# Where loads, casts and sums stand near changes of stage, in a two-sequence encoder on one core

## The chip, the core and the metric

The kernel runs on one core of a Trainium2 chip. The metric is the device time of one execution in microseconds. Three timed runs of the kernel before gave a median of 1177.14 us (1176.59 to 1180.3).

## The reference

A trunk of two layers is applied to two sequences with shared weights: the short one, Q, has 512 positions, the long one, S, has 1024; both have 1024 channels, in float32.

```python
def even_layer(x, ...):                  # layer 1
    p = rms_norm(x, g_norm) @ w_in
    a_val, a_glu, f_in, a_z, f_z = split(p)          # 512 channels each
    a = depthwise_conv(a_val * sigmoid(a_glu), 31)
    a = silu(layer_norm(a)) * silu(a_z)
    f = einsum(fft2(f_in by 4 groups).real, w_four) * silu(f_z)
    return x + concatenate([a, f]) @ w_out

def odd_layer(x, ...):                   # layer 2
    u, bg, cg, z = split(rms_norm(x, g_norm) @ w_in)  # 1024 channels each
    v = depthwise_conv(cg * u, 3)
    return x + ((bg * v) * silu(z)) @ w_out

y = rms_norm(odd_layer(even_layer(x)), final_norm)
```

## The kernel before, in words

Activations lie with channels on the 128 partitions, in chunks of 512 positions: Q is one chunk, S two. Every operand of a product is split into a high and a low part in a reduced float32 format (`split`, L113, and `wsplit`, L143): ACT casts the high part, and a subtraction on DVE (activations) or POOL (weights) makes the low one. A tile of 128 output channels by 512 positions is then 3 x 8 = 24 matmuls (`project`, L174; high by high, high by low, low by high). Weights come in by DMAs of 256 KB that SP issues (`wraw`).

For S, the output projection of layer 1 and the input projection of layer 2 take both chunks and two weight tiles together, as a product of 2 x 2 blocks with seven multiplications instead of eight (`Pair`, L682): a product is 12 matmuls, the products are taken in the order 1, 5, 2, 6, 7, 4, 3, and accumulate in three PSUM tiles X, Z and Y. The weight side needs four sums of raw weight tiles (`sums`, L712, tiles `as` in the ring "T" of eight buffers), the activation side seven operands per block (`keep_op`, L809). X is reused: after products 1 and 6 it is read out into `xr` (layer 1, on DVE, L855) or `mc` (layer 2, on ACT by `taken`, L929) before the next product is added in it. The four pairs of layer 1's output are ma = 0, 2, 4, 6; the one with ma = 2 loads its raw weights early, into the ring "ld" (`room="ld"`).

The order of layer 1: GLU, Fourier input and the gates az and fz of Q and S, one after another. `l1_fz` makes the four fz tiles of Q, of which the last three are made just ahead of S's GLU (L1144); in S's first GLU (`l1_glu`, L343, j = 0) the tile of chunk 0 comes first, then that of chunk 1, which needs the normalised chunk 1: `x` is scaled on DVE (L285), cast to `nh` on ACT and subtracted to `nl` on DVE. The Fourier tables of S (`fourier_tables`, loads `tb`, casts `tbh`, subtractions `tbl`) follow in the program.

From then on a list of steps (`run`, L773) goes through: the layer 2 input tiles of Q for j = 0 to 5 (`l2_in`), the four pairs of layer 1's output for S, Q's tiles j = 6 and 7, Q's output (`l2_out`, tiles named `one` in PSUM), S's layer 2 pairs (`l2_two`), S's output. Side jobs are generators that advance at given steps: `out_ops_a/b/c` make the operands for the pairs of layer 1; `get_acts` (L1020) loads Q's normalised activations (parked in DRAM as `hm`, loaded as `ac`) and splits them to `ysh` and `ysl` for j = 6 and 7; `y2_acts_q` (also `ac`, from `yd`) does so for Q's output; `l2_ops` (L879) normalises S, makes the operands of products 1, 5, 2, 6, 7 and parks those of 4 and 3 in DRAM (`bd`); `prep_far` (L916) loads these (`bf`) and splits them (`bfh`, `bfl`); `l2_out` loads the residual tiles `xr2` and stores the sums (`x2`).

A list scheduler orders the instructions of each engine by simulated time and priority. `order` (L332) adds a dependency that sets the order of issue only. `pace` (L128) uses it: an instruction is placed behind the last evacuation of PSUM that `run` has seen.

Of the kernel before, what the change touches and what calls it, by code (L numbers as in the profile page):

```python
# [12 lines left out]
ALU = mybir.AluOpType  # L13
# [4 lines left out]
CH = 512  # L18
HF = 256
D = 1024  # L20
KD = D // P
# [42 lines left out]
def encoder(ctx: ExitStack, tc: tile.TileContext, xp, xs, w1, w1o, w2, w2o, wf4, par, cst, cdft, dft, outp, outs):  # L64
# [17 lines left out]
    def dp(s, width):  # L82
        return pool.tile([P, width], F32, name=nm(s), tag="dp", bufs=4)
# [25 lines left out]
    def tt(out, a, b, op, eng=nc.vector):  # L109
        ins = eng.tensor_tensor(out=out, in0=a, in1=b, op=op)  # L110
        return seen("now", ins) if eng is nc.vector else ins

    def split(src, tag, s, eng=nc.vector, paced=False):  # L113
        hi = pg(tag, s + "h", F32R)
        lo = pg(tag, s + "l", F32R)
        i = nc.scalar.copy(hi, src)
        j = tt(lo, src, hi.bitcast(F32), ALU.subtract, eng)
        if paced:
            pace(j)
        return hi, lo  # L120

    last = {}

    def seen(kind, ins):
        last[kind] = ins
        return ins

    def pace(ins):  # L128

        if "taken" in last:  # L130
            order(ins, last["taken"])

    def wtile(tag="wo"):
        return pool.tile([P, KD * P], F32R, name=nm("wo"), tag=tag, bufs=4)
# [197 lines left out]
    def order(ins, before):  # L332
        tc.add_manual_dep(ins.ins, before.ins.name, NOSYNC, reason="issue order")
# [6 lines left out]
        else:  # L340
            nc.scalar.activation(t, pq, func)

    def l1_glu(seq, h, skew=False, w0=None):  # L343
        for j in range(4):
            if seq is S:
                a = dp("a", seq.T + 2 * HALO)
            else:
                a = pool.tile([P, seq.T + 2 * HALO], F32, name=nm("ap"), tag="ap", bufs=4)
            nc.vector.memset(a[:, 0:HALO], 0.0)
            nc.vector.memset(a[:, HALO + seq.T:], 0.0)  # L350
            sig = [None] * seq.nc

            def do_glu(c, pq=None):
                if pq is None:
                    pq = project("glu", wg, h[c])
                t = sig[c] = pg("T", "sig")
                act_scaled(seq, t, pq, AF.Sigmoid)
                if seq.r is not None:
                    tt(t, t, seq.r, ALU.mult)

            def do_val(c, pq=None):
                if pq is None:
                    pq = project("val", wv, h[c])
                tt(a[:, HALO + c * CH:HALO + (c + 1) * CH], pq, sig[c], ALU.mult)

            if j == 0 and w0 is not None:
                pg_, pv_ = project_pair(w0, h[0])
                do_glu(0, pg_)
                do_val(0, pv_)
                seq.a.append(a)  # L370
                continue
            wg = load_w(w1, 4 + j)
            if skew and j == 0:
                wv = load_w(w1, j)
                for c in range(seq.nc):
                    do_glu(c)
                    do_val(c)
            else:
                for c in range(seq.nc):
                    do_glu(c)  # L380
                wv = load_w(w1, j)
                for c in range(seq.nc):
                    do_val(c)
            seq.a.append(a)
# [156 lines left out]
                if next(g, 0) == 0:  # L541
                    gens.remove(g)

    def l1_fz(seq, h, c, gs=range(4)):
        for g in gs:
            w = load_w(w1, 16 + g)
            pq = project("fz", w, h[c])
            t = pg("T", "fz")
            act_scaled(seq, t, pq, AF.Silu)
            f = seq.y1[c][4 + g]  # L550
            tt(f, f, t, ALU.mult, nc.gpsimd if seq is Q or c == 1 else nc.vector)
            if seq is S:
                seq.y1[c][4 + g] = park(f, "y1")
# [128 lines left out]
    class Pair:  # L682
# [29 lines left out]
        def sums(self):  # L712
            if self.left is None:
                a11, a21, a22, a12 = self.raw
                s1, s2, s3, s4 = [pg("T", "as") for _ in range(4)]
                tt(s1, a21, a22, ALU.add)
                tt(s2, s1, a11, ALU.subtract)
                tt(s3, a11, a21, ALU.subtract)
                tt(s4, a12, s2, ALU.subtract)
                self.left = {1: a11, 5: s1, 2: a12, 6: s2, 7: s3, 4: a22, 3: s4}  # L720

        def weight(self, p):
# [98 lines left out]
    def out_ops_b(seq, ops):  # L821

        for i in range(4):
            b11, b12 = [ld("y1", seq.y1[c][4 + i]) for c in range(2)]
            b21, b22 = [seq.y1[c][i] for c in range(2)]
            keep_op(ops, 2, b21, "ys", tag="H")
            tt(b12, b22, b12, ALU.subtract)
            keep_op(ops, 7, b12, "ys", tag="FQ")
            tt(b11, b12, b11, ALU.add)
            keep_op(ops, 6, b11, "ys", tag="H")  # L830
            tt(b21, b21, b11, ALU.subtract)
            yield 1
# [8 lines left out]
    def l1_out_two(seq, ops):  # L841
        acc = seq.sm2 = [SqSum(), SqSum()]

        def job(ma):
            at = {11: (0, ma), 12: (1, ma), 21: (0, ma + 1), 22: (1, ma + 1)}

            res = {}

            def pre():
                for ij in (11, 22, 12, 21):  # L850
                    c, m = at[ij]
                    res[ij] = pool.tile([P, CH], F32, name=nm("xr"), tag="ap", bufs=4)
                    nc.sync.dma_start(res[ij], seq.x[m, c])

            def before(ij):  # L855
                def run(x):
                    tt(res[ij], x, res[ij], ALU.add)
                    return res[ij]
                return run

            def after(ij):
                c, m = at[ij]

                def run(x, t=None):
                    t = res[ij]
                    tt(t, x, t, ALU.add)
                    sp = dram.tile([P, CH], F32, name=nm("x1d"), tag=f"x1d{seq.tag}{c}{m}", bufs=1)
                    nc.sync.dma_start(sp, t)
                    seq.x1[c][m] = sp
                    acc[c].add(t)  # L870
                return run

            return Pair(ops, w1o, ma, ma + 1, {ij: before(ij) for ij in (11, 12, 22)}, {ij: after(ij) for ij in at}, True,
                        wide=ma == 6, pre=pre, room="ld" if ma == 2 else None)

        return [job(ma) for ma in range(0, KD, 2)]
# [52 lines left out]
    def taken(tag):  # L929
        def run(x):  # L930
            t = pool.tile([P, CH], F32, name=nm("mc"), tag=tag, bufs=4) if tag == "ap" else pg(tag, "mc")
            nc.scalar.copy(t, x)  # L932
            return t
        return run

# [82 lines left out]
            yield 1  # L1018

    def get_acts(parked, acts, tag):  # L1020
        ts = [ld("ac", d) for d in parked[:4]]
        yield 1
        for n in range(0, KD, 4):
            new = []
            for i, t in enumerate(ts):
                acts.append(split(t, tag, "ys"))
                if n == 0:
                    new.append(ld("ac", parked[4 + i]))
            ts = new
            yield 1  # L1030

    def y2_acts_q(parked, acts):
# [2 lines left out]
                acts.append(split(parked[k] if k == KD - 1 else ld("ac", parked[k]), "F", "ys"))  # L1035
            yield 1

    def l2_out(seq, c, act, acc, ms, spilled=None, halves=None):
        def tile_of(m):
            def run(x):  # L1040
                t = ld("xr2", seq.x1[c][m], "ld" if halves is None else "FQ")
                tt(t, x, t, ALU.add)
                acc.add(t)
                if halves is None:
                    spilled.append(park(t, "x2"))
                else:
                    for h in range(2):
                        halves[h].append(t[:, h * HF:(h + 1) * HF])
            return One(w2o, m, act, run, kind=int(m == 0))
        return [tile_of(m) for m in ms]  # L1050
# [61 lines left out]
        nc.sync.dma_start(d, t)  # L1112
        return d

    def ld(s, src, tag="ld"):
        t = pg(tag, s)
        nc.sync.dma_start(t, src)
        return t


# [20 lines left out]
    second = norm_in(S, 1)  # L1141
    l1_fz(Q, hq, 0, range(1))
    hs.append(norm_in_rest(S, 1, *second))
    l1_fz(Q, hq, 0, range(1, 4))  # L1144
    l1_glu(S, hs, True)
    fourier_tables(S)
    l1_fin(S, hs)
    conv31(Q)
# [14 lines left out]
    def two_norms():  # L1163
# [15 lines left out]
        [t for j in range(n1) for t in l2_in(Q, hm, j, parked, j == 0)],  # L1179
        l1_out_two(S, yo),  # L1180
        [t for j in range(n1, KD) for t in l2_in(Q, hm2, j, parked, j == n1)],
        l2_out(Q, 0, act_q, acc_q, range(KD), out_q),
        [x for j in range(KD) for x in l2_two(S, ops, j)],
        l2_out(S, 0, act_s[0], acc_s[0], range(KD), out_s),
        l2_out(S, 1, act_s[1], acc_s[1], range(nd), halves=xt_e),
    ]
    at, seq = [], []
    for some in parts:
# [3 lines left out]
    run(seq, [  # L1192
        (4, 1, out_ops_a(S, yo)), (8, (0, 2, 4, 5, 6, 7, 8, 9, 10, 11, 12), two_norms()),
        (at[1], 1, out_ops_c(S, yo)),
        (at[2] - 6, 1, get_acts(kept, hm2, "H")),
        (at[2] + 1, (0, 1, 2, 4, 5, 8, 9, 10, 11), l2_ops(S, ops, far)),
        (at[2] + 2, (0, 1, 2, 3, 6), y2_acts_q(parked, act_q)),
        (at[4], 1, prep_far(ops, far)),
        (at[4] + 6, 1, norm_out(Q, 0, acc_q, out_q, "ld")),
        (at[5] - 4, 1, y2_acts(S, 0, act_s[0], "H")),  # L1200
        (at[5] + 1, 1, y2_acts(S, 1, act_s[1], "H")),
# [66 lines left out]
```

## Time and profile before

| | us |
|---|---|
| median of the timed runs | 1177.14 |
| the profiled execution | 1175.05 |
| its span | 1173.2 |
| PE busy | 1133.5 (97%) |
| DVE busy | 858.3 (73%) |
| ACT busy | 469.2 (40%) |
| POOL busy | 538.7 (46%) |

The rows of the profile's views name a line, an engine, an operation, and output <- inputs by the program's tile names, with the number of instructions. A timeline row begins with its start and its length in us; in brackets stands how long the engine was idle before, and what ended that idle time. On SP the rows are issues of DMAs, which include the time in which SP waits for the first of them to be allowed. A row of the waits gives PE's tile and line, the engine and tile waited for, the total, the count and the longest.

### The profile page before, as it was taken

Reading aid. Unit: us, or ns where it says so; the run is one execution under the profiler, and the core shown is the slowest. Engines: PE = TensorE matmul, PEld = TensorE weight load, DVE = VectorE, ACT = ScalarE, POOL = GpSimd, SP = SyncE. Lnnn points to the kernel's source line nnn. Section 1 sums busy time; section 2 is a strip of 40 time slices with the busy share of each in tenths; the row PEclk is TensorE's granted clock in tenths of the full one; section 3 lists DMA queues with packets and bytes.
Section 4 is the critical chain, followed back from the end, with each engine's and each line's share of the span. In section 5 each row is a group of like instructions: output and inputs, shape, how many; then the busy total and the mean of one; then the engine's idle time right before and its main releaser. Section 6 shows DMA issues by size and latency. Waiting matters only on the chain. (4 is left out here: it accounts for less than half of the span.)

```text
span 1173.2 us, 15069 instructions
## 1 busy us (share of the span) xinstructions
PE 1133.5 (97%) x5208; PEld 934.7 (80%) x5208; DVE 858.3 (73%) x1202; ACT 469.2 (40%) x821; POOL 538.7 (46%) x448
## 2 busy tenths in 40 slices
PE   7999989999999999999999999899999999999995
PEld 6778868888988888887778787678888888888895
DVE  6899998999899984878756679675464546455465
ACT  6543532232343354454424444443333243344431
POOL 3452642132256555535644444445444454544551
PEclk9999999999999999999999999999999999999998
DMA  9324211111235575436555756663222222124853
GB/s 343 116 90 126 90 54 44 47 54 55 91 100 169 187 241 191 135 111 189 167 189 195 229 176 219 214 202 112 81 73 72 72 80 73 37 95 147 280 168 128
DMA packets 89212, 159.63 MB, mean 136 GB/s; under 512 B 9904, under 2 KB 13488, under 8 KB 89136
## 3 DMA queue, kind: packets, MB, share of 16 engines
q1 hardware_dynamic: 88848, 158.37, 41.3%
q8 instruction: 41, 0.67, 0.2%
q14 instruction: 35, 0.29, 0.1%
q10 hardware_dynamic: 288, 0.30, 0.1%
HBM read 127.96 MB, written 30.67 MB: 135 GB/s over the span
## 5 line engine op out<-in xcount | busy, mean ns | idle before, releaser
L145 POOL TENSOR_TENSOR wo<-wf,wo 128x512 fp32r<-128x512 f32 x274 | 377.1, 1393 | 445.3 <-ACT wo L144 310.9
L144 ACT CAST wo<-wf 128x512 fp32r<-128x512 f32 x276 | 161.5, 618 | 225.6 <-PE X L738 42.3
L145 POOL TENSOR_TENSOR wo<-as,wo 128x512 fp32r<-128x512 f32 x80 | 111.8, 1397 | 121.5 <-ACT wo L144 120.4
L561 DVE SCALAR_TENSOR_TENSOR cv<-a,par_sb,cv 128x1024 f32<-128x1024 f32 x120 | 154.3, 1285 | 6.9 <-ACT cv L559 4.6
L188 PE MATMUL one<-ysh,wo 128*128 128x512 f32 x432 | 110.6, 393 | 1.9 <-ACT wo L144 1.6
L144 ACT CAST wo<-as 128x512 fp32r<-128x512 f32 x80 | 49.6, 620 | 140.7 <-PE X L738 86.1
L188 PE MATMUL one<-nh,wo 128*128 128x512 f32 x384 | 93.9, 391 | 2.8 <-ACT wo L144 2.8
L188 PEld LDWEIGHTS one<-ysh,wo 128*128 128x128 f32 x432 | 80.5, 188 | 20.2 <-ACT wo L144 2.4
L561 DVE SCALAR_TENSOR_TENSOR cv<-ap,par_sb,cv 128x512 f32<-128x512 f32 x120 | 90.2, 752 | 2.7
L738 PE MATMUL X<-bsh,wo 128*128 128x512 f32 x256 | 85.6, 395 | 2.3 <-ACT mc L932 2.3
L188 PEld LDWEIGHTS one<-nh,wo 128*128 128x128 f32 x384 | 71.9, 188 | 18.7 <-ACT wo L144 3.6
L110 DVE TENSOR_TENSOR acc<-acc,sq 128x512 f32<-128x512 f32 (+1 forms) x77 | 72.3, 944 | 19.1 <-ACT sq L280 18.0
L738 PEld LDWEIGHTS X<-bsh,wo 128*128 128x128 f32 x256 | 48.7, 190 | 13.4 <-ACT mc L932 2.7
L188 PE MATMUL one<-ysl,wo 128*128 128x512 f32 x216 | 58.3, 390 | 0.5 <-DVE ysl L110 0.5
L738 PE MATMUL X<-bsl,wo 128*128 128x512 f32 x128 | 50.8, 397 | 0.0
L188 PE MATMUL one<-nl,wo 128*128 128x512 f32 x192 | 49.3, 392 | 0.0
L188 PEld LDWEIGHTS one<-ysl,wo 128*128 128x128 f32 x216 | 40.6, 188 | 9.4 <-DVE ysl L110 0.9
L738 PE MATMUL Z<-bsh,wo 128*128 128x512 f32 x128 | 44.7, 392 | 0.0
L110 DVE TENSOR_TENSOR mc<-X,mc 128x512 f32<-128x512 f32 x24 | 16.6, 692 | 38.3 <-PE X L738 38.3
L738 PE MATMUL X<-ysh,wo 128*128 128x512 f32 x128 | 41.9, 392 | 2.7 <-DVE xr L110 2.7
L110 DVE TENSOR_TENSOR mc<-Z,mc 128x512 f32<-128x512 f32 x16 | 11.1, 692 | 45.4 <-PE Z L738 45.4
L738 PE MATMUL Z<-bfh,wo 128*128 128x512 f32 x128 | 42.4, 392 | 1.0 <-ACT wo L144 1.0
(310 smaller groups left out, 2480.1 us busy)
## 6 DMA issues: line engine op xcount, KB each, us to landing
wf<-w SPq DMA_DIRECT2D x224, 256.0 KB, 2.9
wf<-w2o SPq DMA_DIRECT2D x48, 256.0 KB, 3.6
wf<-w1o SPq DMA_DIRECT2D x32, 256.0 KB, 3.1
x1d<-xr SPq DMA_DIRECT2D x24, 256.0 KB, 2.8
x1r<-x1d SPq DMA_DIRECT2D x24, 256.0 KB, 3.4
xr<-x1d SPq DMA_DIRECT2D x19, 256.0 KB, 4.0
x<-xs SPq DMA_DIRECT2D x16, 256.0 KB, 5.4
y<-y SPq DMA_DIRECT2D x16, 256.0 KB, 3.9
```

The source lines that it names most:

```text
L110: ins = eng.tensor_tensor(out=out, in0=a, in1=b, op=op)
L144: nc.scalar.copy(hi, t)
L145: eng.tensor_tensor(out=lo, in0=t, in1=hi.bitcast(F32), op=ALU.subtract)
L188: nc.tensor.matmul(out[:, 0:width], a[k], act[k][b][:, cols], start=(n == 0), stop=(n == 3 * KD - 1))
L561: nc.vector.scalar_tensor_tensor(out=acc, in0=src[:, t:t + n], scalar=col(w0 + t), in1=acc, op0=ALU.mult, op1=ALU.add)
L738: nc.tensor.matmul(out, self.w[p][a][:, k * P:(k + 1) * P], self.ops[p][k][b], start=(first and n == 0), stop=(n == 11), skip_group_check= ...
```

## The change

Six things are moved; the work itself is the same but for the number of table loads on ACT.

1. The fourth fz tile of Q (g = 3) is made between chunk 0 and chunk 1 of S's first GLU (`between`). Its weights lie in the ring "F".
2. The four weight sums of the pair ma = 2 are placed behind the first pair's first readout of X (`seen("opened")`).
3. The loads of `y1` in `out_ops_b` are paced.
4. `get_acts` loads all eight tiles of `hm` at once, four in the ring "ld" and four in two wide tiles, starts one step earlier and splits two tiles a step; loads and splits are paced.
5. `prep_far` starts three steps earlier, with its splits four steps later. So that its first loads find room in "ld", Q's `xr2` tiles go to the ring "T".
6. A paced split places its cast behind the last copy of X or Z on ACT too (`seen("copied")`).

```diff
@@ split
         if paced:
             pace(j)
+            pace(i, "copied")
@@
-    def pace(ins):
-        if "taken" in last:
-            order(ins, last["taken"])
+    def pace(ins, kind="taken"):
+        if kind in last:
+            order(ins, last[kind])
@@ l1_glu, the branch with skew
                 for c in range(seq.nc):
                     do_glu(c)
                     do_val(c)
+                    if c == 0 and between:
+                        between()
@@ Pair.sums
-                tt(s1, a21, a22, ALU.add)
-                tt(s2, s1, a11, ALU.subtract)
-                tt(s3, a11, a21, ALU.subtract)
-                tt(s4, a12, s2, ALU.subtract)
+                for o, a, b, op in ((s1, a21, a22, ALU.add), (s2, s1, a11, ALU.subtract),
+                                    (s3, a11, a21, ALU.subtract), (s4, a12, s2, ALU.subtract)):
+                    i = nc.vector.tensor_tensor(out=o, in0=a, in1=b, op=op)
+                    if self.room:
+                        pace(i, "opened")
@@ out_ops_b
-            b11, b12 = [ld("y1", seq.y1[c][4 + i]) for c in range(2)]
+            b11, b12 = [ld("y1", seq.y1[c][4 + i], paced=True) for c in range(2)]
@@ l1_out_two
-                    tt(res[ij], x, res[ij], ALU.add)
+                    i = tt(res[ij], x, res[ij], ALU.add)
+                    if (ij, ma) == (11, 0):
+                        seen("opened", i)
@@ taken
-            nc.scalar.copy(t, x)
+            seen("copied", nc.scalar.copy(t, x))
@@ get_acts
-        ts = [ld("ac", d) for d in parked[:4]]
+        ts = [ld("ac", d, paced=True) for d in parked[:4]]
+        for n in (4, 6):
+            wide = dp("ac", 2 * CH)
+            for h in range(2):
+                ts.append(wide[:, h * CH:(h + 1) * CH])
+                pace(nc.sync.dma_start(ts[-1], parked[n + h]))
         yield 1
-        for n in range(0, KD, 4):
-            new = []
-            for i, t in enumerate(ts):
-                acts.append(split(t, tag, "ys"))
-                if n == 0:
-                    new.append(ld("ac", parked[4 + i]))
-            ts = new
+        for n in range(0, KD, 2):
+            for t in ts[n:n + 2]:
+                acts.append(split(t, tag, "ys", paced=True))
             yield 1
@@ l2_out
-                t = ld("xr2", seq.x1[c][m], "ld" if halves is None else "FQ")
+                t = ld("xr2", seq.x1[c][m], room)
@@ the program
-    l1_fz(Q, hq, 0, range(1, 4))
-    l1_glu(S, hs, True)
+    l1_fz(Q, hq, 0, range(1, 3))
+    l1_glu(S, hs, True, None, lambda: l1_fz(Q, hq, 0, [3], "F"))
@@ parts of the step list
-        l2_out(Q, 0, act_q, acc_q, range(KD), out_q),
+        l2_out(Q, 0, act_q, acc_q, range(KD), "T", out_q),
@@ side jobs
-        (at[2] - 6, 1, get_acts(kept, hm2, "H")),
+        (at[2] - 7, (0, 2, 3, 4, 5), get_acts(kept, hm2, "H")),
-        (at[4], 1, prep_far(ops, far)),
+        (at[4] - 3, (0, 4, 5, 6, 7, 8), prep_far(ops, far)),
```

How this moves instructions, at three places that the prediction speaks of. First DVE, around the first readout of X in the pair ma = 0 (`xr_5106<-X_5157` before, `xr_5108<-X_5159` after); the sums of the pair ma = 2 are `as_5277` to `as_5280` before and `as_5279` to `as_5282` after. Before:

```order
L110 TENSOR_TENSOR as_5277<-wf_5201,wf_5203 128x512
L110 TENSOR_TENSOR as_5278<-as_5277,wf_5199 128x512
L110 TENSOR_TENSOR as_5279<-wf_5199,wf_5201 128x512
L110 TENSOR_TENSOR as_5280<-wf_5205,as_5278 128x512
L110 TENSOR_TENSOR y_989_5139<-one_5114,v_5054 128x512
L110 TENSOR_TENSOR ysl_5150<-a_1370,ysh_5149 128x512
L110 TENSOR_TENSOR ysl_5154<-a_1499,ysh_5153 128x512
L110 TENSOR_TENSOR as_5436<-wf_5374,wf_5376 128x512
L110 TENSOR_TENSOR xr_5106<-X_5157,xr_5106 128x512
```

And after:

```order
L721 TENSOR_TENSOR as_5100<-wf_5025,as_5098 128x512
L110 TENSOR_TENSOR y_991_5141<-one_5116,v_5056 128x512
L110 TENSOR_TENSOR ysl_5152<-a_1331,ysh_5151 128x512
L110 TENSOR_TENSOR ysl_5156<-a_1501,ysh_5155 128x512
L110 TENSOR_TENSOR xr_5108<-X_5159,xr_5108 128x512
L110 TENSOR_TENSOR ysl_5177<-a_1630,ysh_5176 128x512
L721 TENSOR_TENSOR as_5279<-wf_5203,wf_5205 128x512
L110 TENSOR_TENSOR ysl_5181<-a_1759,ysh_5180 128x512
L721 TENSOR_TENSOR as_5280<-as_5279,wf_5201 128x512
L721 TENSOR_TENSOR as_5281<-wf_5201,wf_5203 128x512
```

The four sums, and the first sum of the next pair (`as_5436` before), stand behind the readout of X and mix with the subtractions `ysl`.

Second, ACT at the last pair of layer 1's output (`wo_5693<-wf_5469` is the cast of the weights of Z's last product before, `wo_5731<-as_5598` and `wo_5701<-wf_5471` are among the last pair's casts after; `ysh<-ac` are the casts of Q's parked activations). Before:

```order
L144 CAST wo_5643<-as_5594 128x512
L116 CAST ysh_5714<-ac_5677 128x512
L116 CAST ysh_5746<-ac_5700 128x512
L116 CAST ysh_5750<-ac_5706 128x512
L144 CAST wo_5668<-as_5595 128x512
L116 CAST ysh_5754<-ac_5712 128x512
L116 CAST ysh_5758<-ac_5718 128x512
L144 CAST wo_5693<-wf_5469 128x512
```

And after:

```order
L145 CAST wo_5684<-as_5597 128x512
L145 CAST wo_5701<-wf_5471 128x512
L145 CAST wo_5731<-as_5598 128x512
L281 ACTIVATE sq_5621<-xr_5503 128x512
L281 ACTIVATE sq_5642<-xr_5501 128x512
L281 ACTIVATE sq_5728<-xr_5662 128x512
L145 CAST wo_5785<-wf_5734 128x512
L145 CAST wo_5785<-wf_5736 128x512
L116 CAST ysh_5704<-ac_5648 128x512
L116 CAST ysh_5708<-ac_5650 128x512
```

All casts of `ac` stand behind the pair's weight casts and behind the casts of the next tile's weights (`wo_5785`).

Third, ACT at the first pair of S's layer 2 (`mc_6768<-X_6755` is its first copy of X). Before:

```order
L116 CAST bfh_6773<-bf_6747 128x512
L144 CAST wo_6741<-wf_6435 128x512
L144 CAST wo_6744<-as_6698 128x512
L280 ACTIVATE sq_6736<-xr_1364_6733 128x512
L116 CAST bfh_6779<-bf_6749 128x512
L116 CAST bfh_6811<-bf_6751 128x512
L932 COPY mc_6768<-X_6755 128x512
L144 CAST wo_6770<-as_6699 128x512
L116 CAST bfh_6817<-bf_6753 128x512
```

And after:

```order
L281 ACTIVATE sq_6744<-xr_1368_6741 128x512
L938 COPY mc_6768<-X_6755 128x512
L145 CAST wo_6770<-as_6707 128x512
L116 CAST bfh_6773<-bf_6622 128x512
L116 CAST bfh_6779<-bf_6624 128x512
L938 COPY mc_6798<-Z_6785 128x512
L145 CAST wo_6800<-wf_6435 128x512
L116 CAST bfh_6811<-bf_6626 128x512
L116 CAST bfh_6817<-bf_6628 128x512
```

Before, three casts of far operands stand ahead of the first copy of X; after, none does.

More of the change, by code (lines that the diff above doesn't have):

```diff
@@ L341, in act_scaled, with l1_glu @@
             nc.scalar.activation(t, pq, func)
-    def l1_glu(seq, h, skew=False, w0=None):
+    def l1_glu(seq, h, skew=False, w0=None, between=None):
         for j in range(4):
@@ L542, in interleave, with l1_fz @@
                     gens.remove(g)
-    def l1_fz(seq, h, c, gs=range(4)):
+    def l1_fz(seq, h, c, gs=range(4), tag=None):
         for g in gs:
-            w = load_w(w1, 16 + g)
+            w = load_w(w1, 16 + g, tag)
             pq = project("fz", w, h[c])
@@ L1036, in y2_acts_q, with l2_out @@
             yield 1
-    def l2_out(seq, c, act, acc, ms, spilled=None, halves=None):
+    def l2_out(seq, c, act, acc, ms, room, spilled=None, halves=None):
         def tile_of(m):
             def run(x):
-                t = ld("xr2", seq.x1[c][m], "ld" if halves is None else "FQ")
+                t = ld("xr2", seq.x1[c][m], room)
                 tt(t, x, t, ALU.add)
@@ L1113, in park, with ld @@
         return d
-    def ld(s, src, tag="ld"):
+    def ld(s, src, tag="ld", paced=False):
         t = pg(tag, s)
-        nc.sync.dma_start(t, src)
+        i = nc.sync.dma_start(t, src)
+        if paced:
+            pace(i)
         return t
@@ L1181, in encoder @@
         [t for j in range(n1, KD) for t in l2_in(Q, hm2, j, parked, j == n1)],
-        l2_out(Q, 0, act_q, acc_q, range(KD), out_q),
+        l2_out(Q, 0, act_q, acc_q, range(KD), "T", out_q),
         [x for j in range(KD) for x in l2_two(S, ops, j)],
-        l2_out(S, 0, act_s[0], acc_s[0], range(KD), out_s),
-        l2_out(S, 1, act_s[1], acc_s[1], range(nd), halves=xt_e),
+        l2_out(S, 0, act_s[0], acc_s[0], range(KD), "ld", out_s),
+        l2_out(S, 1, act_s[1], acc_s[1], range(nd), "FQ", halves=xt_e),
     ]
```

## The prediction

> **What bounds the kernel now.** I read the busy shares first, then what PE waits for, then windows around those waits, then the timelines of the engines named there. The page's first part:
>
> ```profile
> span 1173.2 us, 15069 instructions
> PE 1133.5 (97%) x5208; PEld 934.7 (80%) x5208; DVE 858.3 (73%) x1202; ACT 469.2 (40%) x821; POOL 538.7 (46%) x448
> ```
>
> PE is the bound: 1173.2 - 1133.5 = 39.7 us of the span are not PE work, and no edit here removes matmuls. Everything the change can win is in those 39.7 us and in matmuls that run at a lower clock. The waits of PE (wait, releaser, total us, times, longest):
>
> ```profile
> PE one L188 <- ACT wo L144: 4.4, 4, 1.5
> ...
> PE glu L188 <- ACT nh L116: 2.9, 1, 2.9
> PE Z L738 <- ACT wo L144: 2.9, 2, 1.9
> PE X L738 <- DVE xr L110: 2.7, 2, 1.9
> PE X L738 <- ACT mc L932: 2.3, 1, 2.3
> ...
> PE Z L738 <- DVE bfl L110: 1.6, 1, 1.6
> ```
>
> All but a part of the first row lies at stage changes that the diff touches. Five windows around them (PE, PEld, DVE, ACT, POOL busy, then granted clock, DMA share, GB/s) and the long stretch behind:
>
> ```profile
> 150.00:160.00 10.00, 6.96 (x18) 3.96 (x18) 9.89 (x16) 5.21 (x9) 1.41 (x2) 0.83 0.00 0
> 580.00:590.00 10.00, 7.15 (x28) 4.61 (x27) 10.00 (x15) 3.13 (x7) 2.77 (x2) 1.00 0.43 147
> 640.00:660.00 20.00, 17.18 (x74) 13.55 (x73) 14.02 (x20) 8.65 (x16) 6.34 (x5) 1.00 0.78 255
> 700.00:750.00 50.00, 47.91 (x209) 38.59 (x208) 45.12 (x59) 22.64 (x41) 28.38 (x18) 1.00 0.70 231
> 750.00:780.00 30.00, 25.16 (x103) 19.36 (x103) 19.45 (x39) 12.00 (x22) 11.29 (x8) 0.94 0.56 177
> 780.00:1070.00 290.00, 290.00 (x1275) 239.08 (x1274) 156.93 (x189) 108.26 (x181) 138.24 (x104) 1.00 0.26 88
> ```
>
> From 780 to 1070 PE has no gap at all, so a microsecond won earlier arrives at the end whole. In two windows the clock is below 1 too. What that costs is read from start times: at about 773 two matmuls start 0.42 us apart, at 161.7 they start 0.24 apart.
>
> ```profile
> 773.30 0.63 PE L738 MATMUL X<-bsl,wo 128*128 128x512 f32 x1
> 773.72 0.57 PE L738 MATMUL X<-bsh,wo 128*128 128x512 f32 x1
> ```
>
> ```profile
> 161.72 0.39 PE L188 MATMUL glu<-nl,wo 128*128 128x512 f32 x1
> 161.96 0.39 PE L188 MATMUL val<-nl,wo 128*128 128x512 f32 x1
> ```
>
> The window 750 to 780 has a mean clock of 0.94: (1 - 0.94) x 30 = 1.8 us, about eight matmuls with 0.2 us lost on each; I take 1.7.
>
> **The change part by part.**
>
> *The tile between the input chunks (glu wait, 2.94 us at 152.3).* The fourth fz tile of Q moves from ahead of S's first GLU to behind chunk 0's val: its matmuls fill PE where it waits for the casts of chunk 1. But PE's work ahead of chunk 1 is the same sum before and after; the wait is set by DVE, which is full there (9.89 of 10 us).
>
> ```profile
> 153.80 5.35 DVE L285 SCALAR_TENSOR_TENSOR x<-x,par_sb,r 128x512 f32<-128x512 f32 x8
> 159.07 0.75 DVE L561 SCALAR_TENSOR_TENSOR cv<-ap,par_sb,cv 128x512 f32<-128x512 f32 x1
> 159.73 3.69 DVE L110 TENSOR_TENSOR nl<-x,nh 128x512 fp32r<-128x512 f32 x6
> ```
>
> ```profile
> 143.95 1.28 ACT L341 ACT_TABLE_LOAD   x1
> ```
>
> In the new order one fz row and two subtractions of Fourier tables (the shape of nl, 3.69 / 6 = 0.61 each) fall behind the eight x rows instead of ahead: x starts 3 x 0.61 = 1.8 us earlier, so 2.94 becomes 1.1. They now stand between x and nl, so nl starts at about 159.8 as before, and PE, early with the hi parts, waits for the lo parts. The rest of that tile is paced by nl: seven rows at 0.61 us against two matmuls of 0.23 each. The clock lost in this window, (1 - 0.83) x 10 = 1.7 us, fell into that pacing too, since nl was there only just in time. I take a gain of 0.5; bounds 0 and 2.94 + 1.7 = 4.6, the lower end by far the nearer. Two more table loads on ACT come with it, 2 x 1.28 = 2.6 us on an engine that is busy 5.21 of 10 us: nothing; were the idle time gone, one of them would stand ahead of a sigmoid that PE doesn't wait for until a tile later.
>
> *The sums of the pair that starts fourth weights early (the longer X<-xr wait, 1.9).* In the window 580 to 590 DVE is busy all 10 us and PE 7.15, so 2.85 idle. Four sums stand ahead of the accumulator's evacuation:
>
> ```profile
> 575.02 1.78 DVE L110 TENSOR_TENSOR as<-wf,wf 128x512 f32<-128x512 f32 x1
> 576.84 0.69 DVE L110 TENSOR_TENSOR as<-as,wf 128x512 f32<-128x512 f32 x1
> 577.45 0.68 DVE L110 TENSOR_TENSOR as<-wf,wf 128x512 f32<-128x512 f32 x1
> 578.05 1.78 DVE L110 TENSOR_TENSOR as<-wf,as 128x512 f32<-128x512 f32 x1
> ...
> 583.16 0.68 DVE L110 TENSOR_TENSOR xr<-X,xr 128x512 f32<-128x512 f32 x1
> ```
>
> ```profile
> 583.98 0.47 PE L738 MATMUL X<-ysh,wo 128*128 128x512 f32 x1 [1.86 <-DVE xr L110]
> ```
>
> These four (4.93 us) and the one sum of the next pair just ahead of xr (0.68) go behind it: xr at about 577.5, and the wait of 1.86 goes. What is late next is the last lo parts of `a`, which still need the same DVE work and come at about 590; PE has eight matmuls of the next pair (8 x 0.23 = 1.8 us) to put there. Of the 2.85 I take 1.8; bounds 0.5 and 2.9.
>
> *The parked acts of Q (waits at 646.5 and 651.9).* The cast of weights for Z stands on ACT behind a cast of `ac` that waits for its load, and SP stands 5.14 us in four loads ahead of the next xr load:
>
> ```profile
> 644.75 0.62 ACT L116 CAST ysh<-ac 128x512 fp32r<-128x512 f32 x1 [4.32 <-DMA ac<-hm]
> 645.27 0.62 ACT L144 CAST wo<-wf 128x512 fp32r<-128x512 f32 x1
> ```
>
> ```profile
> 641.30 5.14 SPq L1117 DMA_DIRECT2D ac<-yd  x4
> ```
>
> Now all `ac` casts follow the last pair's weight casts, and the four loads follow the xr loads: the 20 - 17.18 = 2.82 us that PE idles in the window 640 to 660 go. New is that all eight loads of `ac` go out together behind those xr loads, shortly before PE wants the first. At the 255 GB/s of this window 256 KB take 1.03 us each, and PE uses one up in three matmuls, 0.7 us: over eight it falls behind by 8 x 0.33 = 2.6, of which the twelve matmuls of the pair's last product that stand among them (2.7 us) cover most. I take 2.0; bounds -2 (all 2.6 and a late first one of 2.2) and 2.8.
>
> *Far operands and the ring of the x1 tiles (waits at 760 to 769).* The copy that frees X stands on ACT behind a cast that waited 4.23 us for `bf`, and four `bf` loads leave SP only at 761.85:
>
> ```profile
> 761.14 0.62 ACT L116 CAST bfh<-bf 128x512 fp32r<-128x512 f32 x1 [4.23 <-DMA bf<-bd]
> 761.66 0.58 ACT L932 COPY mc<-X 128x512 f32<-128x512 f32 x1
> ```
>
> ```profile
> 761.85 1.74 SPq L1117 DMA_DIRECT2D bf<-bd  x4
> ```
>
> In the new order the copy is ahead of every `bfh` cast, and the first four loads each lie soon after their own store, far ahead. The waits of 2.3, 1.0 (the shorter Z<-wo) and 1.6 go, 30 - 25.16 = 4.84 in the window, and the slow stretch behind them (1.7) with them; for the second four loads, which take the place of the late ones, I leave 0.5: a gain of 6.0, bounds 4.0 and 6.5. The trace has the slow stretch start after idle pieces of which none is above 2.3 us, and near 156 after one of 2.94. The Trainium skill ("TensorE: Matmul & The Clock Gate", section "What's actually happening") has the clock halve only after at least one idle window of about 3.4 us. By that rule neither pause would bring a slow stretch, something else would, and the gain here would be 4.3; the trace, with 2.94 us in front of one, does not agree.
>
> *What it costs at 700 to 750.* The early `bf` loads need room, so the xr2 tiles move to the ring of eight that the `as` sums use: a sum now waits until a tile's store has landed, with everything behind it on DVE. On SP two `bf` loads now stand directly behind the store of the same data and hold the weight loads of the output tiles back:
>
> ```profile
> bd<-x1r SPq DMA_DIRECT2D x8, 256.0 KB, 2.8
> ```
>
> So SP stands about 2.8 us at each. DVE is at 90% there, PE idles 2.09 us. Three sums also fall behind evacuations, which helps. Net I take -1.0; bounds -4 and +1.5.
>
> The paced loads of `y1` stand at the same place of SP's order as before, so the two `one` waits near 550, up to 1.5 each, stay: 0.
>
> **Sum:** 0.5 + 1.8 + 2.0 + 6.0 - 1.0 = 9.3. The profiled execution took 1175.05 us (span 1173.2 and 1.85 around it); less 9.3 it is 1165.75. The median of the timed runs, 1177.14, is 2.1 above it: 1167.8, stated as 1168.
>
> **The rivals.**
>
> *Given back before 750 (0.22).* DVE, at 45.12 of 50 us, carries the norm, the far sums and the evacuations. If it and not PE sets when 750 is reached, the 3.8 us won at 580 and 650 only lengthen waits there: 1168 + 3.8 = 1171.8, and about 1174 with a dearer ring. For it: DVE's share. Against: the waits of `one` are for ACT's weights, not for DVE, and DVE's chain is itself started by PE's output.
>
> *The eight loads are late (0.08).* The lower bound above holds, 2.0 becomes -2: 1172. For it: the DMA share of 0.78 in that window.
>
> *Slower (0.05).* A head-of-line wait on SP: each of the two `bf` loads holds the weights of an output tile for 2.8 us, a PE pause of about that size brings a slow stretch of 1.7 as at 156, so 2 x 4.5 = 9; three sums that wait for stores (about 2.8 each) add 8.4 on a full DVE. Together 17.4 instead of 1.0: 1168 + 16.4 = 1184. It decides once the stretch 700 to 750 loses over 13.7 us (1180.7 of the bound below, less 1168, and the 1.0 already counted). For it: 0.70 of DMA share; against: weights are loaded a tile ahead of use, so 2.8 us seldom reach PE.
>
> *The slow stretches stay (0.08).* If the clock drops for another reason than these waits, 1.7 is not won: 1169.7. This is what the skill's rule quoted above would give; 2 of 2 slow stretches right behind the longest groups of waits speak against it.
>
> *The tile fills the glu wait entirely (0.07).* If nl is not what PE waits for, 2.94 + 1.7 is won instead of 0.5: 1164. For it: it is the longest wait here; against: DVE at 9.89 of 10.
>
> That a part does nothing is what I forecast for the y1 loads; the other four change the order on ACT, DVE and SP.
>
> **How the numbers follow.** The forecast keeps 0.50. A measurement can tell 0.3%, 3.5 us: faster is below 1173.6, slower above 1180.7. The bounds on the good side, not all at once, reach to about 1162. Of the first rival a third lies above 1173.6, and the loads' case and the forecast's poor tail add some: same 0.13, slower 0.05, faster 0.82. The range 1162 to 1175 leaves out the slower case, the worst of the first rival, and a little below.
>
> **What would show it.** Right: in the profile after, window 750 to 780 shifted by some 3 us with PE above 29 of 30 us and the clock at 1; no X<-xr wait near 580; no Z<-wo wait near 645. The glu wait shrinks to about 1 and a wait for nl of 1 to 2.5 us appears. Wrong: new waits of `one` for wo between 690 and 750 above 3 us in sum, DVE waits of `as` for a store, or `one` waiting for ysh at 650 above 2 us.

## The result and the profile after

The changed kernel takes 1166.87 us in the median (1166.3 to 1169.29, four runs), the kernel before, on the same chip, 1177.47 us (1176.59 to 1180.3, four runs): a ratio of 0.9921, 95% interval 0.9903 to 0.9939. The forecast of 1168 was 1.1 us off. The page's first part now:

```profile
span 1165.6 us, 15047 instructions
PE 1135.6 (97%) x5208; PEld 936.4 (80%) x5208; DVE 864.1 (74%) x1202; ACT 470.9 (40%) x823; POOL 539.3 (46%) x448
```

PE is busy 2.1 us longer at the same 5208 matmuls, so some of them ran slower; its time without work is 1165.6 - 1135.6 = 30.0 us instead of 39.7. The waits of PE, of the rows that answer to those of before (waiter, releaser, total, times, longest):

```profile
PE one L189 <- ACT wo L145: 2.8, 3, 1.5
PE glu L189 <- DVE nl L110: 2.1, 2, 1.2
...
PE Z L742 <- DVE ysl L110: 1.5, 2, 1.1
PE glu L189 <- ACT nh L116: 1.2, 1, 1.2
PE one L189 <- DVE ysl L110: 0.7, 1, 0.7
```

The waits X<-xr, X<-mc, Z<-wo and Z<-bfl are no longer there; glu<-nl is new, and Z<-ysl has grown from 0.5. By stage (PE, PEld, DVE, ACT, POOL busy, clock, DMA share, GB/s):

```profile
150.00:160.00 10.00, 8.76 (x30) 4.75 (x29) 9.86 (x16) 5.82 (x10) 1.29 (x1) 1.00 0.00 0
160.00:170.00 10.00, 7.87 (x24) 5.21 (x24) 9.89 (x14) 2.85 (x5) 2.95 (x2) 0.83 0.34 106
580.00:590.00 10.00, 9.33 (x42) 7.29 (x40) 10.00 (x12) 4.47 (x8) 4.31 (x4) 1.00 0.40 110
590.00:600.00 10.00, 9.13 (x32) 6.91 (x33) 7.95 (x11) 2.38 (x4) 3.99 (x3) 0.83 0.63 203
640.00:660.00 20.00, 19.88 (x87) 15.93 (x87) 14.20 (x20) 11.06 (x20) 8.17 (x6) 1.00 0.65 221
690.00:740.00 50.00, 48.85 (x214) 39.80 (x213) 44.17 (x65) 22.91 (x41) 26.05 (x17) 1.00 0.74 249
740.00:780.00 40.00, 39.94 (x177) 32.25 (x177) 33.47 (x51) 18.35 (x32) 23.77 (x16) 1.00 0.52 175
```

The stretch at 640 has 0.12 us idle left of 2.82, that at 740 to 780 has 0.06 left (750 to 780 had 4.84 before) and its full clock back. The stretch at 150 to 170 idles 3.37 us, a little more than the 20 - 16.96 = 3.04 of before:

```profile
150.00:170.00 20.00, 16.96 (x60) 11.72 (x60) 17.65 (x28) 9.26 (x16) 8.86 (x5) 0.91 0.10 32
```

All the signs that the prediction names for being right are there. Of its signs for being wrong one is there, a DVE wait of `as` for a store (0.98 us, below); `one` waits only 0.44 us for weights between 690 and 750, and not for `ysh` at 650.

The two profiled executions differ by 1173.2 - 1165.6 = 7.6 us, less than the medians of the runs. Part of that is at a place whose order the change leaves alone. The same ten microseconds, first of the kernel before, then after:

```profile
85.00:95.00 10.00, 7.96 (x44) 6.69 (x43) 10.00 (x19) 6.70 (x12) 2.50 (x2) 1.00 0.49 157
```

```profile
85.00:95.00 10.00, 7.96 (x37) 6.76 (x36) 10.00 (x18) 6.23 (x11) 2.50 (x2) 0.83 0.49 153
```

PE idles the same 2.04 us, but one execution has a clock of 0.83 behind it (seven matmuls fewer in the window, 1.7 us). Of fourteen profiles in this study twelve have this stretch; the profile that the prediction was worked from was one of the two without, and a second profile of the kernel after the other.

### The profile page after: what moved, and what is told of

It is laid out like the page before. It is cut to its first block, busy times and chain, and to the rows that moved or that the text cites. A ratio compares the mean times of both kernels' runs of the same rounds, so it can differ in the third digit from the quotient of the medians.

```text
span 1165.6 us, 15047 instructions
## 1 busy us (share of the span) xinstructions
PE 1135.6 (97%) x5208; PEld 936.4 (80%) x5208; DVE 864.1 (74%) x1202; ACT 470.9 (40%) x823; POOL 539.3 (46%) x448
## 5 line engine op out<-in xcount | busy, mean ns | idle before, releaser
L110 DVE TENSOR_TENSOR acc<-acc,sq 128x512 f32<-128x512 f32 (+1 forms) x77 | 76.3, 999 | 23.2 <-ACT sq L281 22.5
L742 PE MATMUL Y<-bh,wo 128*128 128x512 f32 x128 | 42.4, 392 | 0.0
L189 PEld LDWEIGHTS one<-nl,wo 128*128 128x128 f32 x192 | 36.0, 188 | 7.9 <-issue 0.5
```

The costliest lines, as they stand in the source:

```text
L189: nc.tensor.matmul(out[:, 0:width], a[k], act[k][b][:, cols], start=(n == 0), stop=(n == 3 * KD - 1))
L742: nc.tensor.matmul(out, self.w[p][a][:, k * P:(k + 1) * P], self.ops[p][k][b], start=(first and n == 0), stop=(n == 11), skip_group_check= ...
```

## The experiments

The first four put one part of the change alone on the kernel before.

**The fz tile between the chunks.** Here, as in all of these, the rest is the kernel before:

```diff
-    l1_fz(Q, hq, 0, range(1, 4))
-    l1_glu(S, hs, True)
+    l1_fz(Q, hq, 0, range(1, 3))
+    l1_glu(S, hs, True, None, lambda: l1_fz(Q, hq, 0, [3], "F"))
```

> The kernel before with the fz tile between the input chunks alone. Theory (DVE sets this stage, and table subtractions and the fz row ahead of nl make nl later): the glu wait for nh shrinks from 2.94 to about 1.2, waits for nl of about 2.1 us appear, and the stage ends 0 to 2 us later than before; time within 1177 to 1179.5. Rival (the tile fills the wait): no wait for nl, the stage ends 2.9 to 4.6 us earlier, time about 1173. The prediction's own term was 0.5 faster.

Measured: 1177.77 us, a ratio to before of 0.9992 (0.9978 to 1.0005). The waits are 1.25 for nh and 1.18 + 0.95 for nl. The rival falls: the tile fills one wait and opens another, and the stretch at 150 to 170 idles 3.37 us as in the kernel after.

**The parked activations.**

```diff
-        (at[2] - 6, 1, get_acts(kept, hm2, "H")),
+        (at[2] - 7, (0, 2, 3, 4, 5), get_acts(kept, hm2, "H")),
```

and `get_acts` as the change has it, with eight paced loads at once and paced splits.

> The kernel before with the new order of Q's parked activations alone (eight loads together, paced, casts behind the last pair's weight casts). Theory (head of line on ACT and SP was all of it): the window around 640 to 660 loses its 2.8 us of PE idle, nothing waits for the eight loads, time 3 to 3.5 us under before. Rival (eight loads together are late): PE waits for ysh or ysl of at least 1 us at the first tile j = 6, gain 1 or less.

Measured: 1178.58 us, 1.0001 (0.9986 to 1.0015): nothing won, and my theory fell. The window 640 to 664, here and in the kernel after:

```profile
640.00:664.00 24.00, 21.01 (x90) 16.37 (x90) 12.56 (x19) 11.80 (x21) 7.73 (x6) 1.00 0.76 264
```

```profile
640.00:664.00 24.00, 23.88 (x105) 19.23 (x105) 16.21 (x23) 11.93 (x22) 9.73 (x8) 1.00 0.72 252
```

PE idles 2.99 us here. The rival's gain of 1 or less came true, but not for its reason: PE waits 0.38 us for `ysl`, 1.18 for weights whose low part POOL makes, and, the largest piece, 1.43 for xr. SP's timeline (start, length, line, issue) shows why xr is late:

```profile
647.23 1.87 SPq L1118 DMA_DIRECT2D ac<-hm  x4
649.14 2.11 SPq L1026 DMA_DIRECT2D ac<-hm  x4
651.35 1.39 SPq L853 DMA_DIRECT2D xr<-xs  x2
```

```profile
658.07 0.51 PE L738 MATMUL X<-ysh,wo 128*128 128x512 f32 x1 [1.43 <-DVE xr L110]
```

Two xr loads stand behind the eight ac loads. In the kernel after, one of them stands ahead:

```profile
649.09 0.33 SPq L857 DMA_DIRECT2D xr<-xs  x1
649.47 1.88 SPq L1124 DMA_DIRECT2D ac<-hm  x4
651.39 1.86 SPq L1032 DMA_DIRECT2D ac<-hm  x4
653.29 0.43 SPq L857 DMA_DIRECT2D xr<-xs  x1
```

**The far operands.**

```diff
-        l2_out(Q, 0, act_q, acc_q, range(KD), out_q),
+        l2_out(Q, 0, act_q, acc_q, range(KD), "T", out_q),
-        (at[4], 1, prep_far(ops, far)),
+        (at[4] - 3, (0, 4, 5, 6, 7, 8), prep_far(ops, far)),
```

and the casts of paced splits behind the copies of X and Z.

> The kernel before with the early far loads, the xr2 tiles in the ring T and the casts behind the copies of X alone. Theory: 4.84 us of PE idle between 750 and 780 go and usually the slow stretch behind them, 1 us at most is lost between 700 and 750: 5 to 7 us faster. Rival (the gain needs the rest of the change, since PE reaches this place late or early with the other parts): 3 us or less, with waits of one for wo between 700 and 750 or of X and Z for bfh left.

Measured: 1173.58 us, 0.9957 (0.9939 to 0.9976), which is 5.1 us (2.8 to 7.2). The rival's 3 us lies at the lower end of this. Of its waits, those for `bfh` and `bfl` are down to 0.31 and 0.22 us; `one` waits 2.04 us for weights at 743.9, where the kernel before has 0.66 and 0.92, and the stretch 700 to 750 idles the same (2.04 against 2.09). The window 755 to 780 here, and in only_sums, which lacks this part:

```profile
755.00:780.00 25.00, 24.41 (x109) 19.58 (x108) 21.14 (x38) 11.74 (x22) 11.62 (x9) 1.00 0.47 151
```

```profile
755.00:780.00 25.00, 20.44 (x80) 15.81 (x80) 16.50 (x36) 9.55 (x18) 8.55 (x7) 0.86 0.49 155
```

It is 0.59 us idle against 4.56, and 1.00 against 0.86 in the clock, (1 - 0.86) x 25 = 3.5 us more. The profile of the kernel before has 4.84 and 0.93 there, so half of that loss of clock.

**The weight sums.**

```diff
-                tt(s1, a21, a22, ALU.add)
+                    i = nc.vector.tensor_tensor(out=o, in0=a, in1=b, op=op)
+                    if self.room:
+                        pace(i, "opened")
```

> The kernel before with the four weight sums behind the first readout of X alone. Theory (the wait moves from X to the last lo parts, which need the same DVE work): X<-xr goes (1.86), Z waits for ysl of about 1.5 us appear, the stage wins 0.5 to 1.3; the time is within 1.5 us of before. Rival (prediction's term): 1.8 us faster at the stage and no Z wait over 1 us.

Measured: 1175.51 us, 0.9972 (0.9958 to 0.9986), 3.3 us. At the stage it went as the theory had it: X<-xr is gone, Z waits 1.07 + 0.47 for ysl, 1.3 us of idle less. The time moved by more than the 1.5 us of the theory. One reason that the profile shows is that the window at 640 lost 1.2 us of idle as well (24 - 22.39 = 1.61 left of 2.82), though nothing there was edited; only_fz, which doesn't touch it either, lost 0.8 there. The window in only_sums:

```profile
640.00:664.00 24.00, 22.39 (x99) 18.16 (x98) 14.32 (x22) 12.15 (x22) 9.54 (x8) 1.00 0.77 253
```

**The kernel after again, and three made from it.** The first is unchanged.

> The kernel after once more, as the measure for the three beside it. Theory (which of the waits are followed by a slow stretch of the clock is chance): the same waits of PE as in its first profile within 0.3 us, but the stretches with a clock of about 0.83 in other windows; a ratio to before of 0.990 to 0.994. Rival (each long wait brings its stretch): the stretches in the same windows, 90 to 100, 160 to 170 and 590 to 600.

Measured: 1166.77 us, 0.9915 (0.9901 to 0.9930). The glu, Z and 740 to 780 waits are the same within 0.2 us; the `one` waits are not (below), so the theory held there only in part. The stretches at 90 and 590 are absent this time, that at 160 to 170 is there again. So a wait does not always bring its stretch, and the rival falls; the last section shows what goes with it near 88.

**The fz tile back,** the rest of the change kept:

```diff
-    l1_fz(Q, hq, 0, range(1, 3))
-    l1_glu(S, hs, True, None, lambda: l1_fz(Q, hq, 0, [3], "F"))
+    l1_fz(Q, hq, 0, range(1, 4))
+    l1_glu(S, hs, True)
```

> The kernel after with the fz tile back ahead of S's first GLU; the rest of the change stays. Theory (the tile between the chunks moves the wait from nh to nl and wins nothing): the glu wait is 2.9 again, no wait for nl, the time is that of the kernel after within 1.5 us either way. Rival (the tile wins the 1.7 us by which the nh wait shrank): 2 us slower than the kernel after. Second rival (the tile costs the 2 us that the first pair of profiles shows at this stage): 2 us faster.

Measured: 1165.38 us, 0.9902 (0.9885 to 0.9918): 1.4 us under the kernel after that was measured beside it, with overlapping intervals. The first rival, that the tile wins its 1.7 us, falls; whether it costs one or nothing these runs don't tell.

**The lo parts first.** The fz scaling and the table subtractions are placed behind the last `nl` on DVE:

```diff
@@ norm_apply, after each split
+            if k not in on_pool:
+                seen("lows", last["now"])
@@ fourier_tables, after each split
+                if seq is S:
+                    pace(last["now"], "lows")
@@ act_scaled, for the fz tile between the chunks
+            if late:
+                pace(i, "lows")
```

> The kernel after with the fz scaling and the four table subtractions of S placed behind the nl subtractions, in order of issue. Theory (those rows ahead of nl took what the tile won): the waits for nl of 2.1 us go or fall under 0.7, the nh wait falls under 0.7, the stage is 2 to 3 us shorter, the time 2 to 3 us under the kernel after. Rival (nl is late for another reason, the casts on ACT or POOL): waits for nl stay above 1.5 us.

Measured: 1164.48 us, 0.9899 (0.9884 to 0.9913). DVE in the kernel after and then in this one, where the `nl` rows follow the `x` rows:

```profile
154.33 5.35 DVE L286 SCALAR_TENSOR_TENSOR x<-x,par_sb,r 128x512 f32<-128x512 f32 x8
159.60 0.69 DVE L110 TENSOR_TENSOR tbl<-tb,tbh 128x512 fp32r<-128x512 f32 x1
...
160.86 0.69 DVE L110 TENSOR_TENSOR fz<-fz,rq 128x512 f32<-128x512 f32 x1
161.46 0.86 DVE L110 TENSOR_TENSOR tbl<-tb,tbh 128x512 fp32r<-128x512 f32 x1
162.24 4.77 DVE L110 TENSOR_TENSOR nl<-x,nh 128x512 fp32r<-128x512 f32 x6
```

```profile
153.21 5.35 DVE L286 SCALAR_TENSOR_TENSOR x<-x,par_sb,r 128x512 f32<-128x512 f32 x8
158.48 0.75 DVE L570 SCALAR_TENSOR_TENSOR cv<-ap,par_sb,cv 128x512 f32<-128x512 f32 x1
159.14 3.69 DVE L110 TENSOR_TENSOR nl<-x,nh 128x512 fp32r<-128x512 f32 x6
```

```profile
164.02 0.50 PE L189 MATMUL glu<-nl,wo 128*128 128x512 f32 x1 [0.57 <-POOL nl L110]
```

From the first x to the first nl it is 5.9 us instead of 7.9. Of the waits 1.24 + 1.19 + 0.95 of the kernel after, 0.57 is left, for an nl that POOL makes. For nl the mechanism is shown: the two kernels below that keep this edit have 0.60 left too. For nh it is not: there 1.09 and 1.10 us of the wait stand again. The 2.3 us of time lie inside what the runs scatter.

**All sums behind the operands' lo parts,** on top of lows_first:

```diff
@@ out_ops_c, after each keep_op
+                seen("own", last["now"])
@@ Pair.sums
-                    if self.room:
-                        pace(i, "opened")
+                    pace(i, "own")
```

> lows_first, and with the weight sums of all pairs placed behind the last lo parts of the pairs' own operands instead of the first readout of X. Theory (at 590 PE waits for these lo parts, because sums of both pairs stand between them): the Z<-ysl waits of 1.5 us go, 1 to 2 us faster than lows_first, more where a slow stretch falls away. Rival (the sums are then late): X, Z or Y of the pair ma = 2 wait for wo casts of the sums by at least as much as was won.

Measured: 1167.68 us, 0.9917 (0.9900 to 0.9933). Z<-ysl goes (1.54), a wait of 1.08 for the sums' casts comes at 608, and the stretch at 640 to 664 idles 24 - 20.86 = 3.14 us again: the moved sums brought the xr loads behind the ac loads (ac at 644.76 and 646.67, xr x2 at 648.63).

**Order of the loads alone.** only_acts with the ac loads behind the last xr load:

```diff
+                    seen("xr", nc.sync.dma_start(res[ij], seq.x[m, c]))
+        ts = [ld("ac", d, paced="xr") for d in parked[:4]]
-        (at[2] - 7, (0, 2, 3, 4, 5), get_acts(kept, hm2, "H")),
+        (at[2] - 6, (0, 1, 2, 3, 4), get_acts(kept, hm2, "H")),
```

> only_acts, with all loads of the parked activations behind the last xr load of the last pair in SP's order of issue. Theory (in only_acts what the new order wins is lost again because two xr loads stand behind the eight ac loads on SP): the X<-xr wait of 1.4 us near 658 goes; if the later ac loads then are late, waits of one for ysh or ysl of 1 to 2 us are left, so 1 to 2 us of the 3.0 us idle between 640 and 660 go. Rival (DMA bandwidth and not the order of issue is what is short there): the idle of that window stays at 2.5 to 3.5 us in sum, only its names change.

Measured: 1176.19 us, 0.9990 (0.9973 to 1.0006). SP and the window:

```profile
648.27 0.88 SPq L853 DMA_DIRECT2D xr<-xs  x2
649.20 1.84 SPq L1118 DMA_DIRECT2D ac<-hm  x4
651.09 1.85 SPq L1026 DMA_DIRECT2D ac<-hm  x4
```

```profile
640.00:664.00 24.00, 23.86 (x106) 19.35 (x105) 16.45 (x23) 12.39 (x22) 10.66 (x9) 1.00 0.71 258
```

The idle time goes from 2.99 to 0.14 us with the same eight loads, of which each four still take about 1.9 us to issue and which now start a step later: what PE lacked was the right order of issue, not bandwidth. What that is worth in time is not shown: the ratios of the two, 1.0001 and 0.9990, differ by 1.3 us with overlapping intervals.

**Sums and parked activations together,** the two edits above on the kernel before:

> The kernel before with the moved sums and the new order of the parked activations, and nothing else. Theory (the sums' move shifts the order on SP and DVE so that an xr load comes ahead of the ac loads; the parts only work together): no PE wait over 0.3 us between 640 and 660, as in the kernel after, and 1.5 to 4 us faster than the kernel before with the sums alone at 1175.5, against nothing won by the parked activations alone. Rival (what cures this window in the kernel after is the far part or the fz tile): 1.2 to 3 us idle in this window.

Measured: 1175.65 us, 0.9985 (0.9974 to 0.9996). No wait is left between 640 and 664 (23.88 busy), as the theory had it, and on SP one xr load stands ahead of the ac loads as in the kernel after, so the rival falls. The 1.5 to 4 us of the theory did not come: the time is about that of the sums alone. X<-mc has grown from 1.67 in only_sums to 2.99, which could be the 1.6 us won here, waiting again 110 us later. That is not shown: only_acts, which won nothing here, has 3.29 there.

**The kernel after without the parked activations' part:**

```diff
-        (at[2] - 7, (0, 2, 3, 4, 5), get_acts(kept, hm2, "H")),
+        (at[2] - 6, 1, get_acts(kept, hm2, "H")),
```

> The kernel after with the parked activations loaded and split as before. Theory (with the sums in place this part is worth what it was not worth alone): 1.6 us of X<-xr wait between 640 and 660 as in only_sums, the time 1 to 3 us over the kernel after at 1166.8. Rival (the part is worth nothing there either): within 1 us of the kernel after.

Measured: 1171.38 us, 0.9948 (0.9932 to 0.9965). The wait is larger than the theory had it, 1.12 + 1.96 at 649 and 655, with a slow stretch behind it; by the ratios this part is worth (0.9948 - 0.9915) x 1177 = 3.9 us where the rest is in place (1.3 to 6.5 by the two intervals), so the rival falls.

**lows_own with the loads ordered:** the edits of lows_own and of acts_xr.

> lows_own, with the loads of the parked activations behind the last xr load as in acts_xr. Theory (lows_own lost 3.1 us between 640 and 660 by the order of xr and ac loads on SP, and won 1.5 us at 590): the waits there fall to 1 us or less, 1164 to 1166 us. Rival (they stay, under the names of ysh and ysl): 1167 to 1168.5.

Measured: 1165.63 us, 0.9900 (0.9879 to 0.9921). The stretch at 640 to 664 idles 0.14. lows_first, no_fz and this one came out 1 to 2 us under the kernel after, each within the scatter; none is shown to beat it.

The pacing of the `y1` loads was not run by itself. The two waits of `one` that the prediction expects to stay near 550 are there, 1.27 and 1.53 us before, 0.84 and 1.52 after, 1.39 and 1.52 in after_again.

## Why the prediction was right, term by term

**Far operands: 6.0, held.** Idle fell from 4.84 to 0.06 and the clock of that stretch went back to 1. ACT in the kernel after:

```profile
753.65 0.59 ACT L938 COPY mc<-X 128x512 f32<-128x512 f32 x1 [1.30 <-PE X L742]
754.13 0.62 ACT L145 CAST wo<-as 128x512 fp32r<-128x512 f32 x1
754.65 1.15 ACT L116 CAST bfh<-bf 128x512 fp32r<-128x512 f32 x2
```

The copy now waits for PE and not for a load. Alone it measured 5.1 (2.8 to 7.2). On top of sums and parked activations it is worth more: sums_acts is the kernel after without this part, the tile and the paced `y1` loads, and the ratios differ by 0.9985 - 0.9921 to 0.9985 - 0.9915, which is 7.5 to 8.2 us. The rival that the slow stretches stay falls here: all six profiles without this part (before, only_fz, only_acts, only_sums, acts_xr, sums_acts) have a clock under 1 between 760 and 780, and of the eight with it only own_xr, behind waits of 0.25 and 0.23 us.

**Parked activations: 2.0, right in size for the wrong reason.** PE idle fell by 2.7. The step that failed is that all eight loads of `ac` go out "behind those xr loads": alone (only_acts) all eight stand ahead of two xr loads, and in the kernel after one xr load stands ahead of them and one behind, an order that comes with the moved sums (sums_acts has it too). The four loads of 5.14 us that the prediction shows are not among the eight: they are `ac<-yd`, which another side job, `y2_acts_q`, loads, and they do follow the xr loads now, at 658.54. I priced the danger as eight loads too slow for PE (bandwidth); acts_xr shows them fast enough. Alone the part won nothing that the runs show, with the rest 3.9 us (1.3 to 6.5).

**Sums: 1.8, measured 1.3 of idle.** The wait moved to the last lo parts, as forecast (X<-xr gone, Z<-ysl up by 1.1); in the first profile a slow stretch then took the 1.3 back, in only_sums and after_again it didn't. Alone the time moved by 3.3 us (1.6 to 4.9), of which the stage explains 1.3.

**The tile between the chunks: 0.5, not shown to differ from 0.** The mechanism was as said: nl, not nh, ends the stage. Two things were missed by size: the six nl rows take 4.77 instead of 3.69 us beside a POOL multiplication, and PE idles 3.37 instead of 3.04. only_fz bounds the term to between -0.6 and 2.6 us won.

**700 to 750: -1.0, measured about 0.** The two prices are in the trace, but PE hardly sees them. SP stands before the `bf` load, and a sum waits for a store:

```profile
726.45 0.44 SPq L141 DMA_DIRECT2D wf<-w2o  x1
729.94 0.32 SPq L1124 DMA_DIRECT2D bf<-bd  x1
```

```profile
729.39 0.72 DVE L721 TENSOR_TENSOR as<-as,wf 128x512 f32<-128x512 f32 x1 [0.98 <-DMA x<-xr]
```

SP stood 3.05 us (2.8 forecast), and 1.59 before the next `bf`; the sum stood 0.98. PE waits 0.44 us for weights at 739.7, but not for SP: ACT casts these weights behind casts that waited for DVE, and in the kernel before the same wait was 0.92.

```profile
736.74 0.62 ACT L116 CAST bsh<-x1r 128x512 fp32r<-128x512 f32 x1 [3.81 <-DVE x1r L110]
739.05 1.14 ACT L145 CAST wo<-wf 128x512 fp32r<-128x512 f32 x2
```

PE idled 1.15 us at `one` in this stretch in the first profile and 2.36 in the second, 2.1 before. Neither of the two rivals that start here came: not the slower one, and the gains at 580 and 650 were not given back in the kernel after.

**Sum.** Idle time won, 1.3 + 2.7 + 4.8, with 1.8 of clock and -0.3 at the tile, is 10.3; the ratio says 9.3 (7.2 to 11.4), the forecast said 9.3. That these two agree to the tenth is luck: the terms were off by 0.5 to 1.0 us, some up and some down, and the profile from which they were read was one of the two without a slow stretch near 88.

## What to carry to other kernels

Where an engine takes its instructions in order, a cast or a load that waits for data must not stand ahead of what frees an accumulator; find it as a row with a long idle time in front, directly ahead of the row that PE waits for. A reordering by rules of issue has effects where nothing was edited (with the sums moved, one xr load stands ahead of the ac loads 60 us later), so price a part both alone and with the rest, and pin the order that matters by a rule of its own. A tile that fills a wait wins little if another operand of the next tile comes from the same full engine.

## What the runs showed of the hardware

The clock's slow stretches follow short pauses, and they come on a beat. In all fourteen profiles the granted clock, between start and tail, changes only at whole multiples of 3.41 us from its first change, and a slow stretch is 3.41 or 6.83 us long at a clock of 0.50, so it costs 1.7 us or twice that. Four beats of the kernel before, around its wait for nh:

```profile
149.45:152.86 3.41, 2.75 (x8) 0.98 (x6) 3.27 (x6) 0.81 (x3) 0.00 (x0) 1.00 0.00 0
152.86:156.28 3.42, 1.04 (x4) 0.59 (x4) 3.42 (x6) 1.63 (x3) 0.00 (x0) 1.00 0.00 0
156.28:159.69 3.41, 3.41 (x9) 2.44 (x8) 3.41 (x6) 3.21 (x6) 1.28 (x1) 0.50 0.00 0
159.69:163.10 3.41, 3.41 (x15) 2.45 (x14) 3.41 (x7) 0.11 (x1) 3.22 (x1) 1.00 0.29 88
```

In the second beat PE was busy 1.04 of 3.42 us, and the third ran at half clock. Over the fourteen profiles, up to 1100 us, all 15 full-clock beats in which PE was busy 43% or less were followed by a beat at half clock, 14 of the 42 between 44% and 60%, and 4 of the fuller ones.

What chance there is lies in where the beat falls, which differs from run to run. After the same pauses of 1.76 and 0.28 us near 88, the mean clock from 85 to 100 was 1.00 in two of fourteen profiles, 0.89 in five and 0.77 in seven: 0, (1 - 0.89) x 15 = 1.7 or 3.5 us lost at a place that no part of the change touches. In the two a beat ended 0.45 and 0.47 us behind the longer pause, in the five 1.68 to 2.07, in the seven 0.68 to 1.37; why the seven lose two beats is open. Near 160 the single pause of 2.94 us brought a stretch in seven of seven profiles, the pieces of 1.2 + 1.2 + 0.95 in two of four (both of the kernel after; not only_fz and no_acts). The longest pause, 3.33 us at 588 in only_far, fell across two beats and brought none.

The runs of the unchanged kernel before spread from 1174.86 to 1182.24 us. Over these 30 runs the time falls as the granted clock rises (correlation -0.42; -0.62 over 24 runs on another chip), so the clock is a part of the spread and not all of it; this is why profiles were compared here by idle time and clock apart. The rule of the Trainium skill that the prediction cites ("TensorE: Matmul & The Clock Gate", section "What's actually happening"), that the clock halves after an idle window of about 3.4 us, agrees with these traces in the length of the window and not in its being idle: beats with PE busy up to 43% brought half clock, and between start and tail no pause of PE in any of the profiles was above 3.33 us.
